# First layer's conditioning weights in eighths, summed by TensorE, with idle products in the planned pauses

## The chip, the cores and the metric

The kernel runs on one core of a Trainium2 chip. The metric is device time in microseconds (us): the median over the timed runs of one execution each.

## What is computed

A two-layer streaming encoder over x (2048 frames of 1024 channels, float32), with one conditioning vector c (1024). The part that matters here:

```python
c_act = jax.nn.silu(c)
for i in range(DEPTH):                                   # two layers
    cond = c_act @ ada_w[i] + ada_b[i]                   # ada_w[i]: 1024 x 3072
    shift, scale, gate = cond[:, None, :D], cond[:, None, D:2 * D], cond[:, None, 2 * D:]
    h = rmsnorm(x, norm_g[i]) * (1.0 + scale) + shift
    out = rglru_block(h, ...) if i == 0 else gated_deltanet_block(h, ...)
    x = x + gate * out
return rmsnorm(x, final_g)
```

Both blocks begin with a projection, h @ in_w (1024 x 2048 in the first layer). No projection of a layer can start before its shift and scale are known, and these are sums over all 1024 rows of a weight matrix: shift and scale of the first layer read 8 MB.

## The kernel before

**Tiling.** x is worked on in two halves of 1024 frames, each in two pieces of 512. h is kept with channels on partitions: eight column blocks k of 128 channels, each 128 x 512. The projection weights come in panels of 128 output columns (`raw`, 512 KB). Products are split for precision: weights into a high part `whi` (ScalarE, L701) and a rest `wlo` (VectorE, L707), h likewise into `hh` and `hl` (L622 or L625, and L627). One job is one panel against one piece of 512 frames: three products for each of eight blocks k, 24 matmuls of 128x128 by 128x512, accumulated in one PSUM bank (`mm`, L725). The first four jobs (two panels by two pieces) are interleaved, since each can go on only as far as the blocks of h are there.

**A block of h.** x's frames are loaded (L532), squared and summed by ScalarE (L506), the root taken on GpSimd (L289, L290), scaled by VectorE (L513), transposed by TensorE in blocks of four (`tph`, L547), then ScalarE applies scale and shift (`h`, L617, which waits for `cond` of block k) and the split follows.

**The conditioning columns.** The scale and the shift have to end up with channels on partitions, in `cond`. The 8 MB come in four quarters of 256 channels, each for both parts (part 1 is the scale, part 0 the shift), each in two halves of four row blocks: 16 transfers (`ada`, L346) of 512 KB. The two parts are summed in different ways:

- the scale in `first_pe_thread`: TensorE multiplies c, repeated over 32 columns (`c_bc`), with the raw weights, row blocks j and j+4 in output rows 32j to 32j+31 of one bank (`adaps`, L394); ScalarE copies the bank to `atmp` (L399), and a product with `corner`, a column of ones at rows 0, 32, 64 and 96, adds the four groups and turns 128 channels at a time into a column (L325).
- the shift in `first_dve_thread`: VectorE multiplies the first row block by c and accumulates seven more (`acc`, L418, L420); a product with `ones` adds over partitions (`adac`, L325).

`finish_columns` then adds the bias (L315) and makes g(1 + scale) of the scale (L318). TensorE starts with 40 products of the identity with itself into a bank that nobody reads (`rest`, L379).

**The order.** Nobody writes the order of the instructions by hand. Each piece of work is a generator (a thread of the program `Weave`) that yields the engine that it needs next with a cost in us, an event or a slot of a buffer; the planner always takes the thread that can start first by its own clock, and of equals the one with the higher priority. So costs, priorities and events fix the order in each engine's queue, and on the chip each engine runs its queue strictly in that order. All loads are issued by SP's queue. `SEEDS` scatters the costs by 1%, from another seed every 16 jobs: other seeds give another order for the rest of the program. Each engine's own waits on the chip come on top of the plan.

Of the kernel before, what the change touches and what calls it, by code (L numbers as in the profile page):

```python
# [9 lines left out]
F32 = mybir.dt.float32  # L10
# [3 lines left out]
ALU = mybir.AluOpType  # L14

S = 2048
D = 1024
P = 128
KT = D // P
T = 1024  # L20
NU = S // T
TC = 512
# [54 lines left out]
class Weave:  # L77
    def __init__(self):
        self.free = dict.fromkeys(("pe", "act", "dve", "pool", "sp", "dma"), 0.0)
        self.held = {"dve2": [], "pool2": []}  # L80
        self.table = "exp"
        self.landed, self.through = [0.0] * 8, 0.0
        self.scatter, self.jobs = random.Random(SEEDS[0]), 0
        self.threads = []
        self.now = 0.0

    def count(self):
# [16 lines left out]
    def put(self, slots, token):  # L104
        slots.freed[token] = self.now
# [20 lines left out]
    def engine(self, th, t, kind, dur, lag=None, table=None):  # L126

        e = th.last = kind.rstrip("2")
        if e != "pe":
            dur *= 1.0 + SPREAD * self.scatter.gauss(0.0, 1.0)  # L130
        if table is not None and table != self.table:
            t, self.table = t + TABLE, table
        if kind in SHARED:
            for a, b in self.held[SHARED[kind]][-6:]:
                if a <= t < b:
                    t = b
            self.held[kind].append((t, t + dur + (0.08 if e == "dve" else 0.0)))
        self.free[e] = t + dur
        th.t = t + dur + (LAG[e] if lag is None else lag)

# [36 lines left out]
def trunk_kernel(ctx, tc, x, head, small, ada0, ada_w, ada_b, final_g, w1, gate_w, ow1, w2, wab, ow2, out):  # L177
# [9 lines left out]
    pools = {}  # L187
# [10 lines left out]
    def flat(ap):  # L198
        return ap.rearrange("p a b -> p (a b)")
# [127 lines left out]
    H = TC // 2  # L327

    def first_loads_thread():

        yield ev("firstpanel")
        for q in range(4):
            if q == 1:
                yield ev("firstpanels")
            if q == 3:
                yield ev("loaded", (("in1", 0), 1))
            if q % 2 == 0:
                p = hp if q == 0 else pools["hc"]
                raws = [p.tile([P, KT, TC], F32, tag=f"h{'lh'[part]}{'BC'[q // 2]}", name=f"ada{part}{q}") for part in range(2)]
                raws = [flat(r).rearrange("p (a k c) -> p a k c", a=2, c=H) for r in raws]  # L340
            for part in range(2):
                w.set(ev("adaraw", part, q), raws[part][:, q % 2])
            for g in range(2):
                for part in (1, 0):
                    yield "sp", 1.3, False
                    sp.dma_start(out=raws[part][:, q % 2, 4 * g:4 * g + 4, :], in_=ada0[4 * part + q, :, 4 * g:4 * g + 4, :])  # L346
                    w.spawn(arrive_thread(ev("adaload", part, q, g)), 0)
            w.set(ev("adaissue", q))
# [28 lines left out]
    def idle_products(pt, n):  # L377
        for _ in range(n):
            pe.matmul(pt[:, 0:P], lhsT=ident, rhs=ident, start=True, stop=True)  # L379

    def first_pe_thread():

        rest = ps.tile([P, TC], F32, tag="mm", name="rest")
        idle_products(rest, 40)
        c_bc, ttok = yield ev("cbc")
        for q in range(4):
            raw = yield ev("adaraw", 1, q)
            ctok = yield slots["c"]
            pt = ps.tile([P, H], F32, tag="c", name="adaps")
            for g in range(2):  # L390
# [12 lines left out]
            yield from finish_columns(0, 1, 2 * q, 2, pt[:, 0:2])  # L403
            put("c", ctok)
        put("yf", ttok)

    def first_dve_thread():

        yield ev("c")
        for q in range(4):  # L410
            ttok = yield slots["tz"]
            acc = tile_([P, H], "tz", "acc")
            raw = yield ev("adaraw", 0, q)
# [7 lines left out]
            ctok = yield slots["c"]  # L421
            yield "pe", 0.5
            pt = ps.tile([P, 2], F32, tag="c", name="adac")
            columns_of(acc, pt, 2, ones[:, 0:1])
            put("tz", ttok)
            yield from finish_columns(0, 0, 2 * q, 2, pt)
            put("c", ctok)
        yield ev("cond", 0, 1, KT - 1)
        w.set(ev("ada"))

    def columns_thread():
        neg = tile_([P, KT], "tf1", "neg")
# [229 lines left out]
    def panels_thread():  # L662
        yield ev("small")
        ahead = []
        for name, panels, _ in plans:
            for m, p in enumerate(panels):
# [4 lines left out]
                    yield ev("owt", 1, 1)  # L671
                    yield ev("gates")
                if m == 0 and name == ("in1", 0):
                    yield ev("loaded", (("in1", 0), 0))
                    ahead.append((yield from panel_load(name, panels[0])))
                    w.set(ev("firstpanel"))
                    yield ev("adaissue", 0)
                    ahead.append((yield from panel_load(name, panels[1])))
                    w.set(ev("firstpanels"))
                if m in (2, len(panels) - 1) or m < 2 and name != ("in1", 0):  # L680
                    if name == ("in1", 0):
                        yield ev("adaissue", 3)
# [1031 lines left out]
    with tc.manual_schedule():  # L1714
# [20 lines left out]
        w.spawn(norm_thread((in1[0], 1), 0, x, TC, "B", [ev("adaissue", 2)], [ev("cond", 0, 1, 3), ev("cond", 0, 0, 3)],  # L1735
                            ("yh", "yh", "yl", "yl"), "tg"), 2)
        w.spawn(turned_thread((in1[1], 0), 0, x, T, "C", [ev("adaissue", 3), ev("split", (in1[0], 1), KT - 1)],
                              [ev("turned", (in1[1], 1))], [ev("ada")]), TP)
        w.spawn(turned_thread((in1[1], 1), 0, x, T + TC, "A", [ev("turned", (in1[1], 0))], [ev("loaded", (in1[1], 0))], [ev("free", in1[0], 0)]), TP)
        w.spawn(out_weights_thread(1, ow1, 0, 0.5, "B", [ev("free", in1[0], 1)], []), 3)  # L1740
# [31 lines left out]
def layout(**inputs):  # L1772
# [10 lines left out]
    def table(*parts):  # L1783
# [40 lines left out]
```

## Time and profile before

| | |
|---|---|
| median of 3 timed runs | 1838.78 us (1836.51 to 1843.77) |
| profiled execution | 1842.69 us |
| its span, first to last instruction | 1840.4 us |
| TensorE busy | 1808.1 us, 98% |
| VectorE busy | 1343.7 us, 73% |
| ScalarE busy | 1136.3 us, 62% |

The span is that of one profiled execution, and the views of the trace are about it. Busy time of TensorE is that of pipelined products whose ends are modelled, so two rows can overlap by some tenths of a us; the distance from one start to the next is the better price. A 32-bit product shows as two rows, one for each pass; products of the split parts show as one.

### The profile page before, as it was taken

Reading aid. Unit: us, or ns where it says so; the run is one execution under the profiler, and the core shown is the slowest. Engines: PE = TensorE matmul, PEld = TensorE weight load, DVE = VectorE, ACT = ScalarE, POOL = GpSimd, SP = SyncE. Lnnn points to the kernel's source line nnn. Section 1 sums busy time; section 2 is a strip of 40 time slices with the busy share of each in tenths; the row PEclk is TensorE's granted clock in tenths of the full one; section 3 lists DMA queues with packets and bytes.
Section 4 is the critical chain, followed back from the end, with each engine's and each line's share of the span. In section 5 each row is a group of like instructions: output and inputs, shape, how many; then the busy total and the mean of one; then the engine's idle time right before and its main releaser. Section 6 shows DMA issues by size and latency. Waiting matters only on the chain.

```text
span 1840.4 us, 31168 instructions
## 1 busy us (share of the span) xinstructions
PE 1808.1 (98%) x10350; PEld 1454.5 (79%) x10350; DVE 1343.7 (73%) x3113; ACT 1136.3 (62%) x2683; POOL 359.9 (20%) x895
## 2 busy tenths in 40 slices
PE   8999999999999999999999999999999999999998
PEld 6777776777788878787888788787888888778887
DVE  7889887777554747877788887677766776876653
ACT  4766766666212358686877676776787687664221
POOL 2112001000000003223333231232222232211100
PEclk8999999999999999999999999999999999999999
DMA  9567746555678735667677667456555565686741
GB/s 360 140 192 208 241 158 193 159 180 164 205 211 226 225 103 150 161 164 171 165 188 174 153 146 226 117 148 161 147 135 140 148 155 137 163 261 186 249 139 69
DMA packets 510424, 322.74 MB, mean 175 GB/s; under 512 B 369844, under 2 KB 437940, under 8 KB 510264
## 3 DMA queue, kind: packets, MB, share of 16 engines
q1 hardware_dynamic: 510264, 320.77, 62.7%
q8 instruction: 81, 1.33, 0.3%
q14 instruction: 79, 0.65, 0.1%
HBM read 219.93 MB, written 100.73 MB: 174 GB/s over the span
## 4 chain that ended last, share of the span: by engine, by line
PE 71%; DVE 10%; DMA 6%; ACT 5%; issue 4%; SPq 3%; POOL 1%; DVEq 0%; POOLq 0%; ACTq 0%
PE mm L725 39%; PE mmo L725 18%; PE pg L858 3%; DVE xf L778 2%; DMA raw<-in_w 2%; PE py L1451 1%; PE pS L1464 1%; PE pS L1463 1%; PE pp L1434 1%; PE pp L1435 1%; PE pqk L1284 1%; DVE tblk L1319 1%; PE pkk L1196 1%; DVE ttmp L1316 1%; SPq L1531 1%
## 5 line engine op out<-in xcount | busy, mean ns | idle before, releaser
L778 DVE SCALAR_TENSOR_TENSOR xf<-xe,small_s,xf 128x512 f32<-128x512 f32 x288 | 215.1, 751 | 49.9 <-ACT xf L1037 46.3
L701 ACT CAST whi<-raw 128x1024 fp32r<-128x1024 f32 x96 | 100.0, 1041 | 33.0 <-DMA raw<-in_w 29.6
L1316 DVE TENSOR_TENSOR ttmp<-blk,tblk 128x60 f32<-128x60 f32 (+24 forms) x496 | 104.7, 211 | 15.8 <-DMA blk<-blk_d 4.2
L1319 DVE TENSOR_TENSOR tblk<-tblk,ttmp 128x60 f32<-128x60 f32 (+24 forms) x496 | 105.9, 214 | 12.5
L725 PE MATMUL mm<-hh_('in2', 1)_11904,whi 128*128 128x512 f32 x256 | 104.0, 406 | 0.7 <-ACT tz L1052 0.7
L725 PE MATMUL mm<-hh_('in2', 1)_11629,whi 128*128 128x512 f32 x256 | 104.4, 408 | 0.1
L725 PE MATMUL mm<-hl_('in2', 1)_11905,whi 128*128 128x512 f32 x256 | 104.0, 406 | 0.0
L725 PE MATMUL mm<-hh_('in2', 1)_11629,wlo 128*128 128x512 f32 x256 | 103.7, 405 | 0.0
L725 PE MATMUL mm<-hh_('in2', 0)_5185,whi 128*128 128x512 f32 x256 | 103.6, 405 | 0.0
L725 PE MATMUL mm<-hh_('in2', 1)_11904,wlo 128*128 128x512 f32 x256 | 103.5, 404 | 0.0
L725 PE MATMUL mm<-hh_('in2', 0)_5074,wlo 128*128 128x512 f32 x256 | 103.4, 404 | 0.0
L725 PE MATMUL mm<-hl_('in2', 1)_11630,whi 128*128 128x512 f32 x256 | 103.4, 404 | 0.0
L725 PE MATMUL mm<-hh_('in2', 0)_5074,whi 128*128 128x512 f32 x256 | 103.3, 403 | 0.0
L725 PE MATMUL mm<-hh_('in2', 0)_5185,wlo 128*128 128x512 f32 x256 | 103.2, 403 | 0.0
L725 PE MATMUL mmo<-oh,oh 128*128 128x512 f32 (+1 forms) x264 | 103.0, 390 | 0.0
L725 PE MATMUL mm<-hl_('in2', 0)_5186,whi 128*128 128x512 f32 x256 | 102.9, 402 | 0.0
L725 PE MATMUL mm<-hl_('in2', 0)_5075,whi 128*128 128x512 f32 x256 | 102.8, 402 | 0.0
L725 PE MATMUL mmo<-ol,oh 128*128 128x512 f32 (+1 forms) x264 | 102.6, 388 | 0.0
L725 PE MATMUL mmo<-oh,ol 128*128 128x512 f32 (+1 forms) x264 | 102.4, 388 | 0.0
L725 PE MATMUL mmo<-oh,yl 128*128 128x512 f32 x256 | 100.9, 394 | 0.1
L725 PE MATMUL mmo<-oh,yh 128*128 128x512 f32 x256 | 100.8, 394 | 0.0
L725 PE MATMUL mmo<-ol,yh 128*128 128x512 f32 x256 | 100.8, 394 | 0.0
(321 smaller groups left out, 5315.6 us busy)
## 6 DMA issues: line engine op xcount, KB each, us to landing
raw<-in_w SPq DMA_DIRECT2D x96, 512.0 KB, 4.1
araw<-in_ada_w SPq DMA_DIRECT2D x32, 512.0 KB, 4.8
xt<-x_d SPq DMA_DIRECT2D x32, 512.0 KB, 6.0
xt_d<-xb SPq DMA_DIRECT2D x192, 64.0 KB, 2.6
xk<-xt_d SPq DMA_DIRECT2D x24, 512.0 KB, 5.8
xt<-in_x SPq DMA_DIRECT2D x16, 512.0 KB, 6.4
ada<-in_ada SPq DMA_DIRECT2D x16, 512.0 KB, 10.8
y_d<-tz SPq DMA_DIRECT2D x32, 256.0 KB, 3.4
```

The source lines that it names most:

```text
L701: act.copy(hi, raw)
L725: pe.matmul(pt, lhsT=lhs[a][:, k, :], rhs=rhs[b][:, k, :], start=(k == 0 and n == 0), stop=(k == KT - 1 and n == 2))
L778: dve.scalar_tensor_tensor(xf, xe[:, 1 + j:1 + j + TC], wc[:, j:j + 1], xf, ALU.mult, ALU.add)
L858: pe.matmul(pg, lhsT=gw[:, g, :], rhs=xf, start=True, stop=True)
L1196: pe.matmul(pkk[:, b, :], lhsT=kc, rhs=kc, start=True, stop=True)
L1284: pe.matmul(pqk[:, b, :], lhsT=kt[:, b * P:(b + 1) * P], rhs=qt[:, b * P:(b + 1) * P], start=True, stop=True)
L1316: dve.tensor_tensor(tmp, blk[:, j, j + 1:32].unsqueeze(2).to_broadcast([P, r, c_]), t[:, j, 0:c_].unsqueeze(1).to_broadcast([P, r, c_]), A ...
L1319: dve.tensor_tensor(t[:, j + 1:32, 0:c_], t[:, j + 1:32, 0:c_], tmp, ALU.subtract)
L1434: pe.matmul(pp[:, 0, :], lhsT=kc, rhs=S_, start=True, stop=True)
L1435: pe.matmul(pp[:, 1, :], lhsT=qc, rhs=S_, start=True, stop=True)
L1451: pe.matmul(py, lhsT=rm[:, b, :], rhs=zt, start=True, stop=True)
L1463: pe.matmul(pS[:, 0, :], lhsT=kd[:, b, :], rhs=yt, start=True, stop=True)
```

## The change

1. The weights come in eighths: 128 channels of one part with all eight row blocks, 16 transfers of 512 KB as before. `first_loads_thread` issues the first pair right behind x's first piece, then the first panel, a pair, the second panel, two pairs, x's second piece (which waited for three quarters before, and for four eighths now) and the last four pairs.
2. Both parts are summed by TensorE: two `first_pe_thread`, one for each part. An eighth is eight products of 32 x 128 in four column groups, a copy (ScalarE for the scale and the first shift, VectorE for the other seven), one product with `corner` and `finish_columns` for one column. `first_dve_thread` is gone.
3. Idle products: `warm_thread`, with the lowest priority, puts one wherever TensorE is free in the plan, until the first block of h is split. After that `engine` fills each planned pause of TensorE before 45 us of the plan with as many as fit, if an `adaps` bank is open to take them.
4. The seeds are others.

```diff
-SEEDS, SPREAD = (32, 45, 51, 36, 4, 54, 53, 16, 3, 25, 36, 8, 28, 14, 37, 0, 0), 0.01
+SEEDS, SPREAD = (59, 49, 32, 0, 2, 54, 53, 2, 57, 22, 53, 52, 51, 54, 27, 0, 0), 0.01
+IDLE = 45.0
...
+        if e == "pe" and self.idle and t < IDLE:
+            self.idle(int((t - self.free[e] - 0.1) / 0.23))
...
-        yield ev("firstpanel")
-        for q in range(4):
-            if q == 1:
+        yield ev("loaded", (("in1", 0), 0))
+        for e in range(8):
+            if e == 1:
+                yield ev("firstpanel")
+            if e == 2:
                 yield ev("firstpanels")
-            if q == 3:
+            if e == 4:
                 yield ev("loaded", (("in1", 0), 1))
...
-                    sp.dma_start(out=raws[part][:, q % 2, 4 * g:4 * g + 4, :], in_=ada0[4 * part + q, :, 4 * g:4 * g + 4, :])
+                sp.dma_start(out=raws[part][:, e % 4], in_=ada0[8 * part + e])
...
-    def first_pe_thread():
-
-        rest = ps.tile([P, TC], F32, tag="mm", name="rest")
-        idle_products(rest, 40)
+    def warm_thread(stop):
+
+        mtok = yield slots["mm"]
+        pt = ps.tile([P, TC], F32, tag="mm", name="warm")
+        while stop.t is None:
+            yield "pe", 0.43 if w.now < 7.0 else 0.23, 0.0
+            pe.matmul(pt[:, 0:P], lhsT=ident, rhs=ident, start=True, stop=True)
+        put("mm", mtok)
+        w.idle = idle_products
+
+    def idle_products(n):
+
+        if w.rest is not None:
+            for _ in range(n):
+                pe.matmul(w.rest[:, 3 * P:4 * P], lhsT=ident, rhs=ident, start=True, stop=True)
+
+    def first_pe_thread(part, other):
...
-            for g in range(2):
-                yield ev("adaload", 1, q, g)
-                yield "pe", 1.15 if q + g else 2.2, 0.0 if g == 0 else 0.2
-                for j in range(4):
-                    pe.matmul(pt[32 * j:32 * j + 32], lhsT=c_bc[:, 4 * g + j, :], rhs=raw[:, 4 * g + j, :],
-                              start=(g == 0), stop=(g == 1))
+            for k in range(KT):
+                pe.matmul(pt[32 * (k % 4):32 * (k % 4) + 32, 0:P], lhsT=c_bc[:, k], rhs=raw[:, k, :], start=(k < 4), stop=(k >= 4))
             xtok = yield slots["xr"]
-            yield "act", 0.36
-            tmp = tile_([P, H], "xr", "atmp")
-            act.copy(tmp, pt)
-            yield "pe", 0.5
-            columns_of(tmp, pt, 2, corner)
+            tmp = tile_([P, P], "xr", "atmp")
+            if part == 0 and e > 0:
+                yield "dve", 0.2
+                dve.tensor_copy(out=tmp, in_=pt[:, 0:P])
+            else:
+                yield "act", 0.2
+                act.copy(tmp, pt[:, 0:P])
+            yield "pe", 0.25, 0.3
+            pe.matmul(pt[:, 0:1], lhsT=tmp, rhs=corner, start=True, stop=True)
...
-    def first_dve_thread():
-
-        yield ev("c")
-        for q in range(4):
...
-            for k in range(KT):
-                yield ev("adaload", 0, q, k // 4)
-                yield "dve", 0.41
-                if k == 0:
-                    dve.tensor_scalar(acc, raw[:, 0], c_col[:, 0:1], None, ALU.mult)
-                else:
-                    dve.scalar_tensor_tensor(acc, raw[:, k], c_col[:, k:k + 1], acc, ALU.mult, ALU.add)
...
-        w.spawn(first_pe_thread(), 1)
-        w.spawn(first_dve_thread(), 0)
+        w.spawn(warm_thread(ev("split", (in1[0], 0), 0)), 20, 1.0)
+        w.spawn(first_pe_thread(1, 0), 1)
+        w.spawn(first_pe_thread(0, 1), 1)
...
-        "ada0": v["ada_w"][0, :, :2 * D].reshape(KT, P, 8, TC // 2).transpose(2, 1, 0, 3),
+        "ada0": v["ada_w"][0, :, :2 * D].reshape(KT, P, 16, P).transpose(2, 1, 0, 3),
```

The start of TensorE's queue before, up to the first weight product (each row: line, operation, output and operands, size of the output, count; `ada_182` holds quarters of the scale, `tph` are the transposes of x):

```order
L379 MATMUL rest<-ident 128x128 x40
L394 MATMUL adaps<-ada_182,c_bc 32x256 x4
L547 MATMUL tph<-ident,xt 128x128 x4
L394 MATMUL adaps<-ada_182,c_bc 32x256 x4
L547 MATMUL tph<-ident,xt 128x128 x8
L325 MATMUL adaps<-corner,atmp 128x1 x2
L547 MATMUL tph<-ident,xt 128x128 x4
L325 MATMUL adac<-ones,acc 128x1 x2
L394 MATMUL adaps<-ada_182,c_bc 32x256 x4
L547 MATMUL tph<-ident,xt 128x128 x8
L394 MATMUL adaps<-ada_182,c_bc 32x256 x4
L725 MATMUL mm<-hh_('in1', 0)_263,whi 128x512
```

The same start with the change (`ada_141` holds eighths of the scale, `ada_140` of the shift):

```order
L384 MATMUL warm<-ident 128x128 x35
L404 MATMUL adaps<-ada_141,c_bc 32x128 x8
L384 MATMUL warm<-ident 128x128 x3
L404 MATMUL adaps<-ada_140,c_bc 32x128 x8
L414 MATMUL adaps<-corner,atmp 128x1
L384 MATMUL warm<-ident 128x128
L541 MATMUL tph<-ident,xt 128x128 x4
L414 MATMUL adaps<-corner,atmp 128x1
L541 MATMUL tph<-ident,xt 128x128 x4
L384 MATMUL warm<-ident 128x128
L541 MATMUL tph<-ident,xt 128x128 x4
L404 MATMUL adaps<-ada_141,c_bc 32x128 x8
```

The first weight product stands six rows further on, behind the two eighths of the second pair, where it stood behind two quarters of the scale. Up to the first eighth of the second group (`ada_352`) the queue now holds 8 eighths, 8 column sums, 9 idle products besides the first 35, 8 blocks of four transposes and 24 weight products.

The end of the conditioning work in TensorE's queue before (`_263`, `_264` are h of the first piece, `_505`, `_506` of the second):

```order
L394 MATMUL adaps<-ada_254,c_bc 32x256 x4
L547 MATMUL tph<-ident,xt 128x128 x4
L725 MATMUL mm<-hl_('in1', 0)_264,whi 128x512
L725 MATMUL mm<-hh_('in1', 0)_263,wlo 128x512
L325 MATMUL adaps<-corner,atmp 128x1 x2
L725 MATMUL mm<-hh_('in1', 0)_263,whi 128x512
L725 MATMUL mm<-hl_('in1', 0)_264,whi 128x512
L725 MATMUL mm<-hh_('in1', 0)_263,wlo 128x512
L325 MATMUL adac<-ones,acc 128x1 x2
```

And with the change (`_270`, `_271` the first piece, `_527` the second):

```order
L404 MATMUL adaps<-ada_352,c_bc 32x128 x8
L414 MATMUL adaps<-corner,atmp 128x1
L719 MATMUL mm<-hh_('in1', 0)_527,whi 128x512
L719 MATMUL mm<-hh_('in1', 0)_270,whi 128x512
L719 MATMUL mm<-hl_('in1', 0)_271,whi 128x512
L414 MATMUL adaps<-corner,atmp 128x1
L404 MATMUL adaps<-ada_351,c_bc 32x128 x8
L719 MATMUL mm<-hh_('in1', 0)_270,wlo 128x512
L541 MATMUL tph<-ident,xt 128x128 x4
L719 MATMUL mm<-hh_('in1', 0)_270,whi 128x512
L414 MATMUL adaps<-corner,atmp 128x1
```

The last column sum stood behind 36 of the 96 weight products of the first four jobs and 9 of 16 blocks of transposes; it now stands behind 35 and 10. Between the second group's first eighth and it are 8 eighths, 8 column sums, 5 idle products, 11 weight products and 2 blocks. Ahead of it stood a VectorE accumulation; now it is a VectorE copy, which waits for the eighth that TensorE has just done.

## Rows read from the trace of the kernel before

**Rows 1.** The page: busy us (share of the span) and instructions of each engine.

```profile
PE 1808.1 (98%) x10350; PEld 1454.5 (79%) x10350; DVE 1343.7 (73%) x3113; ACT 1136.3 (62%) x2683; POOL 359.9 (20%) x895
```

**Rows 2.** Windows: stretch and length, busy us (instructions) by engine, PEclk, DMA share, GB/s.

```profile
13.37:45.41 32.04, 26.49 (x165) 17.73 (x165) 24.52 (x59) 13.76 (x24) 5.30 (x8) 0.84 0.97 389
36.00:45.41 9.41, 7.47 (x45) 4.36 (x46) 8.64 (x21) 4.13 (x8) 3.98 (x6) 1.00 0.84 337
45.41:66.69 21.28, 21.26 (x101) 16.09 (x102) 19.26 (x39) 15.79 (x26) 1.48 (x4) 1.00 0.11 31
66.69:120.00 53.31, 53.31 (x222) 41.34 (x221) 47.10 (x77) 38.58 (x53) 9.69 (x14) 1.00 0.75 206
66.69:1780.00 1713.31, 1694.87 (x9754) 1364.58 (x9753) 1266.13 (x2955) 1088.97 (x2596) 340.81 (x844) 1.00 0.64 176
```

**Rows 3.** The chain that ended last, 41 to 60 us: start us, us, what.

```profile
41.25 0.75 DVE xt L513
42.00 0.40 DVE acc L420
...
44.88 0.39 DVE acc L420
...
45.41 0.58 PE adac L325 x4
45.99 0.80 PE mm L725 x3
...
48.75 0.44 PE tph L547 x4
...
53.03 6.15 PE mm L725 x27
```

**Rows 4.** The conditioning transfers (L346): issue in ns, first and last start; landing.

```profile
L346 SPq DMA_DIRECT2D ada<-in_ada x16: 328/328/483, 4.3 to 28.8; - x16
...
DMA to landing us min/median/max: 7.8/10.8/11.6
```

**Rows 5.** Groups by line, 0 to 66.7 us: busy us, mean ns | idle before.

```profile
L420 DVE SCALAR_TENSOR_TENSOR acc<-ada,c_col,acc 128x256 f32<-128x256 f32 x28 | 13.5, 483 | 1.2 <-DMA ada<-in_ada 0.6
...
L399 ACT COPY atmp<-adaps 128x256 f32<-128x256 f32 x4 | 1.5, 374 | 8.1 <-PE adaps L394 8.1
...
L418 DVE TENSOR_SCALAR acc<-ada,c_col 128x256 f32<-128x256 f32 x4 | 1.4, 348 | 0.2 <-DMA ada<-in_ada 0.2
...
L315 DVE TENSOR_TENSOR cond<-adaps,head_s 128x2 f32<-128x2 f32 x4 | 0.6, 154 | 1.9 <-PE adaps L325 1.9
```

**Rows 6.** Windows of the idle products (L379) alone: PE, PEld, PEclk, DMA, GB/s.

```profile
1.52:7.25 5.73, 5.73 (x27) 5.73 (x28) 1.00 0.87 280
7.25:13.37 6.12, 6.12 (x55) 5.99 (x54) 1.00 1.02 404
```

**Rows 7.** Windows, columns as in rows 2.

```profile
20.00:35.00 15.00, 13.63 (x76) 9.71 (x77) 10.18 (x25) 7.21 (x13) 0.41 (x2) 0.66 1.03 410
```

**Rows 8.** Timeline, 41 to 46 us: start us, us, instruction, count.

```profile
41.49 0.16 PEld L394 LDWEIGHTS adaps<-ada,c_bc 128*32 128x32 f32 x8 [0.36 <-issue]
41.49 0.64 PE L394 MATMUL adaps<-ada,c_bc 128*32 128x256 f32 x8
...
42.06 0.66 PE L547 MATMUL tph<-ident,xt 128*128 128x128 f32 x4
...
45.85 0.48 PE L725 MATMUL mm<-hh_('in1', 0)_505,whi 128*128 128x512 f32 x1
```

**Rows 9.** Timeline of PE, 19 to 67 us: [idle before <- what ended it].

```profile
19.93 0.64 PE L394 MATMUL adaps<-ada,c_bc 128*32 128x256 f32 x8 [1.05 <-DMA ada<-in_ada]
21.78 1.97 PE L547 MATMUL tph<-ident,xt 128*128 128x128 f32 x8 [1.21 <-ACT h L617]
...
24.69 0.80 PE L725 MATMUL mm<-hh_('in1', 0)_263,whi 128*128 128x512 f32 x1
...
66.69 0.39 PE L725 MATMUL mm<-hh_('in1', 0)_263,whi 128*128 128x512 f32 x1
```

**Rows 10.** PE's waits, 66.69 to 1780 us: us in total, times, longest.

```profile
PE pg L858 <- DMA gw<-in_gate_w: 2.2, 1, 2.2
```

More of the change, by code (lines that the diff above doesn't have):

```diff
@@ L84, in __init__ @@
         self.threads = []
+        self.idle = self.rest = None
         self.now = 0.0
@@ L325, in columns_of @@
             pe.matmul(pt[:, q:q + 1], lhsT=acc[:, q * P:(q + 1) * P], rhs=weights, start=True, stop=True)
-    H = TC // 2
     def first_loads_thread():
-        yield ev("firstpanel")
-        for q in range(4):
-            if q == 1:
+        yield ev("loaded", (("in1", 0), 0))
[3 more added lines that the diff above has]
+            if e == 2:
                 yield ev("firstpanels")
-            if q == 3:
+            if e == 4:
                 yield ev("loaded", (("in1", 0), 1))
[L337 to L342, printed above, removed]
-            for g in range(2):
-                for part in (1, 0):
-                    yield "sp", 1.3, False
-                    sp.dma_start(out=raws[part][:, q % 2, 4 * g:4 * g + 4, :], in_=ada0[4 * part + q, :, 4 * g:4 * g + 4, :])
-                    w.spawn(arrive_thread(ev("adaload", part, q, g)), 0)
-            w.set(ev("adaissue", q))
+            if e % 4 == 0:
+                p = hp if e == 0 else pools["hc"]
+                raws = [p.tile([P, KT, TC], F32, tag=f"h{'lh'[part]}{'BC'[e // 4]}", name=f"ada{part}{e}") for part in range(2)]
+                raws = [flat(r).rearrange("p (a k c) -> p a k c", a=4, c=P) for r in raws]
+            for part in (1, 0):
+                yield "sp", 1.3, False
+                sp.dma_start(out=raws[part][:, e % 4], in_=ada0[8 * part + e])
+                w.spawn(arrive_thread(ev("adaload", part, e), raws[part][:, e % 4]), 0)
+            w.set(ev("adaissue", e))
     def arrive_thread(event, value=True):
@@ L375, in first_small_thread @@
         w.set(ev("cbc"), (c_bc, ttok))
-    def idle_products(pt, n):
-        for _ in range(n):
-            pe.matmul(pt[:, 0:P], lhsT=ident, rhs=ident, start=True, stop=True)
-    def first_pe_thread():
-        rest = ps.tile([P, TC], F32, tag="mm", name="rest")
-        idle_products(rest, 40)
+    def warm_thread(stop):
[3 more added lines that the diff above has]
+            yield "pe", 0.43 if w.now < 7.0 else 0.23, 0.0
+            pe.matmul(pt[:, 0:P], lhsT=ident, rhs=ident, start=True, stop=True)
+        put("mm", mtok)
+        w.idle = idle_products
@@ L385, in first_pe_thread @@
+    def idle_products(n):
[3 more added lines that the diff above has]
+    def first_pe_thread(part, other):
         c_bc, ttok = yield ev("cbc")
-        for q in range(4):
-            raw = yield ev("adaraw", 1, q)
+        for e in range(8):
+            raw = yield ev("adaload", part, e)
             ctok = yield slots["c"]
-            pt = ps.tile([P, H], F32, tag="c", name="adaps")
-            for g in range(2):
-                yield ev("adaload", 1, q, g)
-                yield "pe", 1.15 if q + g else 2.2, 0.0 if g == 0 else 0.2
-                for j in range(4):
-                    pe.matmul(pt[32 * j:32 * j + 32], lhsT=c_bc[:, 4 * g + j, :], rhs=raw[:, 4 * g + j, :],
-                              start=(g == 0), stop=(g == 1))
-            xtok = yield slots["xr"]
-            yield "act", 0.36
-            tmp = tile_([P, H], "xr", "atmp")
-            act.copy(tmp, pt)
-            yield "pe", 0.5
-            columns_of(tmp, pt, 2, corner)
+            yield "pe", 0.46, 0.3
+            pt = ps.tile([P, TC], F32, tag="c", name="adaps")
+            w.rest = pt
+            for k in range(KT):
+                pe.matmul(pt[32 * (k % 4):32 * (k % 4) + 32, 0:P], lhsT=c_bc[:, k], rhs=raw[:, k, :], start=(k < 4), stop=(k >= 4))
+            xtok = yield slots["xr"]
+            tmp = tile_([P, P], "xr", "atmp")
[7 more added lines that the diff above has]
+            pe.matmul(pt[:, 0:1], lhsT=tmp, rhs=corner, start=True, stop=True)
@@ L402, in first_pe_thread @@
             put("xr", xtok)
-            yield from finish_columns(0, 1, 2 * q, 2, pt[:, 0:2])
+            yield from finish_columns(0, part, e, 1, pt[:, 0:1])
+            if w.rest is pt:
+                w.rest = None
             put("c", ctok)
-        put("yf", ttok)
-    def first_dve_thread():
-        yield ev("c")
[L410 to L413, printed above, removed]
-            for k in range(KT):
-                yield ev("adaload", 0, q, k // 4)
-                yield "dve", 0.41
-                if k == 0:
-                    dve.tensor_scalar(acc, raw[:, 0], c_col[:, 0:1], None, ALU.mult)
-                else:
-                    dve.scalar_tensor_tensor(acc, raw[:, k], c_col[:, k:k + 1], acc, ALU.mult, ALU.add)
[L421 to L429, printed above, removed]
@@ L431, in columns_thread @@
+        yield ev("cond", 0, other, KT - 1)
+        if part == 1:
+            put("yf", ttok)
+            w.set(ev("ada"))
     def columns_thread():
@@ L673, in panels_thread @@
                 if m == 0 and name == ("in1", 0):
-                    yield ev("loaded", (("in1", 0), 0))
+                    yield ev("adaissue", 0)
                     ahead.append((yield from panel_load(name, panels[0])))
                     w.set(ev("firstpanel"))
-                    yield ev("adaissue", 0)
+                    yield ev("adaissue", 1)
                     ahead.append((yield from panel_load(name, panels[1])))
@@ L681, in panels_thread @@
                     if name == ("in1", 0):
-                        yield ev("adaissue", 3)
+                        yield ev("adaissue", 7)
                     ahead.append((yield from panel_load(name, p)))
@@ L1734, in trunk_kernel @@
         w.spawn(rows_thread(), 4)
-        w.spawn(norm_thread((in1[0], 1), 0, x, TC, "B", [ev("adaissue", 2)], [ev("cond", 0, 1, 3), ev("cond", 0, 0, 3)],
+        w.spawn(norm_thread((in1[0], 1), 0, x, TC, "B", [ev("adaissue", 3)], [ev("cond", 0, 1, 3), ev("cond", 0, 0, 3)],
                             ("yh", "yh", "yl", "yl"), "tg"), 2)
-        w.spawn(turned_thread((in1[1], 0), 0, x, T, "C", [ev("adaissue", 3), ev("split", (in1[0], 1), KT - 1)],
+        w.spawn(turned_thread((in1[1], 0), 0, x, T, "C", [ev("adaissue", 7), ev("split", (in1[0], 1), KT - 1)],
                               [ev("turned", (in1[1], 1))], [ev("ada")]), TP)
```

## Prediction

> **What bounds the kernel now.** I first read where each engine is busy: TensorE 98% of the span, VectorE 73%, ScalarE 62% [rows 1]. A change at the start is therefore worth the TensorE time that it frees there, if that is not lost again. Next, the stretches [rows 2]. From 13.37 us (the last of the 40 idle products) to 45.41 us, TensorE works 26.49 of 32.04 us; from 45.41 us to 66.69 us, where the fifth job begins [rows 9], 21.26 of 21.28; up to 120 us all of it; up to 1780 us 1694.87 of 1713.31. So from 45.41 us on TensorE hardly waits. The question is what it waits for before, and how much work is left at that moment.
>
> The chain of work shows it [rows 3]: before 45.41 us it runs through VectorE, over the row scales of x's second half (L513) and the weighted sum of the shift columns (L420), into the column sums `adac` (L325). From 45.99 us on it is TensorE alone. Was the data late? The last conditioning transfer was issued at 28.8 us, and such a transfer takes 10.8 us (7.8 to 11.6) to land [rows 4], so it was there at 39.6 us (40.4 at the latest). The last run of accumulations starts at 42.00 us in the chain: VectorE, busy 8.64 of the last 9.41 us, and not the transfers, holds the tail [rows 2, 3].
>
> **The change, part by part.**
>
> *VectorE and ScalarE.* 28 accumulations of 483 ns and four multiplications of 348 ns go, 14.9 us [rows 5]. In come seven copies of 128x128 from PSUM; the trace has none. A two-column operation from PSUM takes 0.15 us on VectorE, ScalarE's copy of twice the columns 0.37 [rows 5]; between these I take 0.25, 1.8 us together. So the VectorE end of the chain goes. ScalarE swaps four copies of 0.37 us for nine, at 0.25 each: +0.8 us, in a stretch where it is idle for 18 of 32 us [rows 2].
>
> *Transfers.* 16 pieces of 0.5 MB stay 16. In the order of SP's queue x's second half moves ahead of four half quarters. The last piece keeps its place, so it lands at 39.6 us again; the piece that opens the second group of eighths comes seven transfers sooner. At the 410 GB/s that DMA moves here [rows 7] a transfer of 524 KB takes 1.28 us: it lands at 39.6 - 9.0 = 30.6 us.
>
> *TensorE, the prices.* An eighth is 8 products of 128 columns, 16 passes; a half quarter was 4 products of 256, 8 passes, in 0.64 us, and the next operation started 0.57 us behind its start [rows 8]. The streamed columns are the same, with four groups of 32 output rows at a time. If that overlap holds, an eighth costs 0.6 us. If it fails, each pass costs what a pass of the idle products costs: 55 of them start in the 6.12 us behind 7.25 us [rows 6], 111 ns each, so 1.78 us. I take 0.6, since eight loads of 32 columns took only 0.16 us [rows 8]. Against me speaks the Trainium skill (TensorE: Matmul & The Clock Gate, section Back-to-back issue gap): it puts a sustained stream of load and product pairs at 81 ns a pair for 128 columns, by which, as an estimate, an eighth is 1.3 us and the kernel ends near 1847. The trace's idle pairs are slower still than that, but its column groups overlap.
> Two column sums held TensorE for 0.44 us (45.41 to 45.85) [rows 3, 8]; one: 0.3 (0.22 to 0.44). A block of four transposes takes 0.44, a weight product 6.15/27 = 0.228 [rows 3]. An idle product is two passes, 0.22; the first 27 passes took 5.73 us, twice as long each, though no lower clock is recorded for them [rows 6].
>
> *TensorE, the sum.* The 35 products of `warm` at the start are 70 passes: 27 until 7.25 us, 43 x 0.111 = 4.8 us more, so they end at 12.0 us. From there to the second group of eighths the order holds 8 eighths (4.8), 8 column sums (2.4), 9 idle products (2.0), 8 blocks (3.5) and 24 weight products (5.5): 18.2 us, to 30.2 us, just when the next piece lands (30.6). From there to the last column sum: 8 eighths (4.8), 8 sums (2.4), 5 idle products (1.1), 11 weight products (2.5), 2 blocks (0.9), 11.7 us: 41.9 us with no wait. By the data alone it is 39.6 + 0.6 + 0.23 + 0.44 + 0.23 + 0.3 = 41.4 us. TensorE is now the later of the two. It will not be free of waits: before, they were 5.5 us of this stretch, two of them over 1 us between 18 and 22 us, for a transfer and for ScalarE [rows 2, 9]. In the new order ScalarE puts the four squares of x's second half between the split of columns 3 and 4, for which products wait. I put 1.5 us (0.4 to 4.5) for all waits: the last column sum ends at 43.4 us, where it ended at 45.99.
>
> *What is left then.* 61 of 96 weight products and 6 blocks, against 60 and 7: 0.23 - 0.44 = -0.2 us. So 43.4 - 45.99 - 0.2 = **-2.8 us** (-4 to +0.5). The first weight product comes much sooner than now (24.69 us [rows 9]), near 18 us; most of that only moves waits behind it.
>
> *The rest of the program.* TensorE is full until 120 us, with VectorE at 88% and the transfers at 75% [rows 2], so what follows starts sooner with it. The other seeds redraw the order of all that is behind; by the two orders the kinds and counts of instructions stay, but for four more ScalarE table loads. Behind 66.69 us TensorE waits 18.44 us [rows 2], the longest time, 2.2 us, for a gate-weight transfer [rows 10]. I cost the new order at nothing, with 4 us either way.
>
> The profiled execution took 1842.69 us, 2.3 above its span and 3.9 above the median of the three timed runs. On its own time the sum gives 1839.9; against the median, 1838.8 - 2.8 = **1836.0 us**.
>
> **The rivals.**
> *The clock falls (the gain is lost).* From 20 to 35 us the mean granted clock was 0.66, part of the time at the lower level of 1.2 GHz: 15 x 0.34 = 5.1 us of TensorE's time [rows 7], right after the two long waits [rows 9]. It cost little then, since TensorE had to wait anyway. The new order has 29.9 us of work in a stretch of 31, so the same fall costs 5.1 us less the 1.0 us of waits that it covers: 43.4 + 4.1, +1.3 us in all, 1840. For it: idle products fill the planned pauses, not those that a late transfer makes. Against: products of weights begin 6 us sooner and the pauses are shorter. It decides from 2.8 us lost, 5.6 us at half clock.
> *Eighths do not overlap (slower).* 16 x (1.78 - 0.6) = 18.9 us on TensorE's path, less 2.8: 1855. From 0.78 us for an eighth the gain is gone, from 1.35 us the kernel is slower by over 0.5%. Against it: the 0.64 us of the half quarter. The pair rate of the Trainium skill's TensorE page (same section) lies between the two.
> *The gain is not carried.* If later waits grow by as much as TensorE arrives sooner: 1838.8. For it: VectorE at 88%; against: a TensorE without a wait until 120 us.
> *The redrawn order decides.* If a third of the later 18.4 us goes, 1836 - 6 = 1830; if half, 1827; likewise upwards.
>
> **How the numbers follow.** Forecast 0.56 (its own range 1832 to 1840); not carried 0.12; clock 0.15; redrawn order by 6 us or more 0.11; eighths that do not overlap, or a clock that stays low through most of the head (24 us of it are needed), 0.06. The range from 1830 to 1844.5 leaves out most of the redrawn order, the slow eighths and a little of the clock. 0.5%, 9.2 us, is about what this measurement can tell from no change: below 1829.6 lies a lucky order (0.08), above 1848 the last case and an unlucky one (0.06), between them 0.86.
>
> **What would show it.** Right: the last column sum near 43 us, the first weight product near 18, the fifth job's first product near 64 us instead of 66.69, a clock of 1.00 from 10 to 45 us, some 0.64 us for the products of an eighth. Wrong: an eighth above 0.8 us, TensorE at the low clock while it is busy, waits for the copies `atmp` between eighths, or a later stretch that differs by more than 3 us.

## The result and the profile after

The changed kernel takes 1847.47 us (median of 7, 1846.3 to 1854.87), the kernel before 1838.73 us (7, 1836.51 to 1843.77): ratio 1.005, interval 1.0036 to 1.0064. So it is slower by 8.7 us, where 1836.0 us was forecast and the range ended at 1844.5. The profiled execution of after took 1846.65 us.

The page of after, row of the busy times, and its windows (columns as in [rows 2]), which answer to [rows 1, 2]:

```profile
PE 1812.9 (98%) x10560; PEld 1461.5 (79%) x10560; DVE 1329.9 (72%) x3100; ACT 1143.0 (62%) x2692; POOL 358.8 (19%) x895
```

```profile
13.37:45.41 32.04, 30.21 (x374) 23.22 (x373) 16.74 (x48) 16.90 (x31) 3.62 (x8) 1.00 0.97 387
36.00:45.41 9.41, 9.28 (x129) 7.00 (x122) 5.74 (x20) 4.12 (x8) 0.00 (x0) 1.00 0.84 336
45.41:66.69 21.28, 21.28 (x99) 16.38 (x99) 19.67 (x39) 16.09 (x27) 2.49 (x5) 1.00 0.15 41
...
1000.00:1200.00 200.00, 192.80 (x1300) 154.73 (x1299) 149.42 (x439) 139.67 (x402) 51.90 (x124) 0.99 0.59 152
```

VectorE has lost its accumulations (16.74 us busy in the head for 24.52), TensorE works 30.21 us of it, and its granted clock is 1.00 throughout. TensorE's timeline of after in the head answers to [rows 8, 9]:

```profile
18.43 0.64 PE L404 MATMUL adaps<-ada,c_bc 128*32 128x128 f32 x16
19.00 0.50 PE L719 MATMUL mm<-hh_('in1', 0)_270,whi 128*128 128x512 f32 x1
...
33.22 0.71 PE L392 MATMUL adaps<-ident 128*128 128x128 f32 x4 [0.38 <-ACT atmp L412]
33.77 0.28 PE L414 MATMUL adaps<-corner,atmp 128*128 128x1 f32 x2
33.98 0.64 PE L404 MATMUL adaps<-ada,c_bc 128*32 128x128 f32 x16
35.03 0.71 PE L392 MATMUL adaps<-ident 128*128 128x128 f32 x4 [0.41 <-DVE atmp L409]
35.68 0.64 PE L404 MATMUL adaps<-ada,c_bc 128*32 128x128 f32 x16
...
39.28 0.49 PE L719 MATMUL mm<-hh_('in1', 0)_270,whi 128*128 128x512 f32 x1
39.60 0.40 PE L719 MATMUL mm<-hl_('in1', 0)_271,whi 128*128 128x512 f32 x1
39.84 0.39 PE L719 MATMUL mm<-hh_('in1', 0)_270,wlo 128*128 128x512 f32 x1
40.06 0.28 PE L414 MATMUL adaps<-corner,atmp 128*128 128x1 f32 x2
...
45.12 0.28 PE L414 MATMUL adaps<-corner,atmp 128*128 128x1 f32 x2
...
65.39 0.40 PE L719 MATMUL mm<-hh_('in1', 0)_270,whi 128*128 128x512 f32 x1
```

The first parts behave much as forecast: 0.64 us for an eighth's 16 passes, the first weight product at 19.00 us (24.69 before, near 18 forecast). The fifth job starts at 65.39 us, 1.3 us sooner than in [rows 9], where 64 was forecast. But the last column sum starts at 45.12 us, against 45.41 before. One reason stands in the rows: the idle products of a planned pause (L392) write the `adaps` bank whose copy is running, and are released by that copy (`<-ACT atmp`, `<-DVE atmp`). They run behind the pause, not in it: 0.71 us for four passes ahead of the next column sum or eighth.

So after leads by 1.3 us at the fifth job and still ends 4.3 us behind before's profiled execution (spans 1844.7 and 1840.4). It changes sides in one stretch: from 1000 to 1200 us TensorE works 192.80 us (row above), in before 196.79:

```profile
1000.00:1200.00 200.00, 196.79 (x1336) 160.06 (x1335) 154.59 (x450) 145.06 (x420) 52.77 (x132) 1.00 0.62 159
```

What happens there in after is shown by SP's queue, the chain of waits and TensorE's timeline, three views of the same 20 us:

```profile
1097.63 1.90 SPq L596 DMA_DIRECT2D xk<-xt_d  x3
1099.63 0.92 SPq L1049 DMA_DIRECT2D z_d<-tz  x2
```

```profile
1099.63 7.84 DMA z_d<-tz
...
1107.55 0.61 ACT tz L1046
...
1108.20 4.00 PE mm L719 x11
```

```profile
1105.26 0.39 PE L719 MATMUL mm<-hh_('in2', 0)_5187,wlo 128*128 128x512 f32 x1
1108.20 0.50 PE L719 MATMUL mm<-hh_('in2', 0)_5187,whi 128*128 128x512 f32 x1 [2.55 <-ACT tz L1046]
...
1109.46 0.60 PE L719 MATMUL mm<-hh_('in2', 0)_5187,wlo 128*128 128x512 f32 x1
1109.86 0.63 PE L719 MATMUL mm<-hh_('in2', 0)_5187,whi 128*128 128x512 f32 x1
```

Three reloads of `xk` stand ahead of two stores of `z_d`. A store lands 7.84 us after its issue; the next `tz` can only then be written, and it releases the PSUM bank for which the product at 1108.20 us waits, 2.55 us. 1.3 us behind the start of that product the products take 0.6 us each: the granted clock is 0.50 for 3.4 us. The same place in before:

```profile
1101.72 0.37 SPq L1055 DMA_DIRECT2D z_d<-tz  x1
1102.13 2.31 SPq L602 DMA_DIRECT2D xk<-xt_d  x3
1104.55 0.40 SPq L1055 DMA_DIRECT2D z_d<-tz  x1
```

One store goes ahead of the reloads, and TensorE has no such wait (its longest from 1080 to 1114 us is 1.43 us, for another operand). The head did not change this queue; the redrawn order did.

### The profile page after: what moved, and what is told of

The parts are those of the page before. It is cut to its first block, busy times and chain, and to the rows that moved or that the text cites. A ratio compares the mean times of both kernels' runs of the same rounds, so it can differ in the third digit from the quotient of the medians.

```text
span 1844.7 us, 31580 instructions
## 1 busy us (share of the span) xinstructions
PE 1812.9 (98%) x10560; PEld 1461.5 (79%) x10560; DVE 1329.9 (72%) x3100; ACT 1143.0 (62%) x2692; POOL 358.8 (19%) x895
## 4 chain that ended last, share of the span: by engine, by line
PE 74%; DVE 9%; ACT 6%; DMA 5%; issue 2%; SPq 2%; POOL 0%; DVEq 0%; POOLq 0%; ACTq 0%
PE mm L719 42%; PE mmo L719 16%; PE pg L852 3%; DVE xf L772 1%; PE py L1445 1%; PE pqk L1278 1%; PE pp L1428 1%; PE pS L1457 1%; PE pS L1458 1%; PE pp L1429 1%; DMA oraw<-in_ow 1%; DVE tblk L1313 1%; PE pkk L1190 1%; DVE ttmp L1310 1%; DMA raw<-in_w 1%
## 5 line engine op out<-in xcount | busy, mean ns | idle before, releaser
L719 PE MATMUL mm<-hh_('in2', 0)_5187,whi 128*128 128x512 f32 x256 | 103.3, 403 | 3.2 <-ACT tz L1046 3.2
L719 PE MATMUL mm<-hh_('in2', 0)_5187,wlo 128*128 128x512 f32 x256 | 104.5, 408 | 0.0
L719 PE MATMUL mm<-hl_('in2', 1)_11740,whi 128*128 128x512 f32 x256 | 104.4, 408 | 0.0
L719 PE MATMUL mm<-hh_('in2', 1)_12016,wlo 128*128 128x512 f32 x256 | 104.3, 407 | 0.0
L719 PE MATMUL mm<-hh_('in2', 1)_11739,whi 128*128 128x512 f32 x256 | 103.6, 404 | 0.7 <-ACT tz L1046 0.7
L719 PE MATMUL mm<-hl_('in2', 0)_5299,whi 128*128 128x512 f32 x256 | 104.1, 407 | 0.0
L719 PE MATMUL mm<-hl_('in2', 1)_12017,whi 128*128 128x512 f32 x256 | 103.8, 406 | 0.0
L719 PE MATMUL mm<-hh_('in2', 0)_5298,whi 128*128 128x512 f32 x256 | 103.7, 405 | 0.0
L719 PE MATMUL mm<-hh_('in2', 1)_11739,wlo 128*128 128x512 f32 x256 | 103.7, 405 | 0.0
L719 PE MATMUL mm<-hl_('in2', 0)_5188,whi 128*128 128x512 f32 x256 | 103.6, 405 | 0.0
## 6 DMA issues: line engine op xcount, KB each, us to landing
ada<-in_ada SPq DMA_DIRECT2D x16, 512.0 KB, 10.2
```

The source lines that it names most:

```text
L719: pe.matmul(pt, lhsT=lhs[a][:, k, :], rhs=rhs[b][:, k, :], start=(k == 0 and n == 0), stop=(k == KT - 1 and n == 2))
```

## The experiments

**Theory:** the redrawn order loses the time, and the head is worth little. **Rivals:** the new head itself costs the time later on (its idle products, or its lead that meets other transfers); or the forecast's base, the profiled execution of before, had an unusual head.

The first four kernels part seeds, head and idle products.

*e1* and *e2* exchange the line of seeds between the two kernels. The diff is that of e1, the changed kernel with the old line; e2 is the kernel before with the new line, the reverse:

```diff
-SEEDS, SPREAD = (59, 49, 32, 0, 2, 54, 53, 2, 57, 22, 53, 52, 51, 54, 27, 0, 0), 0.01
+SEEDS, SPREAD = (32, 45, 51, 36, 4, 54, 53, 16, 3, 25, 36, 8, 28, 14, 37, 0, 0), 0.01
```

> The changed kernel with the old table of seeds. Theory A (the order behind the first jobs, redrawn by plan and seeds, decides; the first jobs themselves gain 1 to 3 us): away from the changed kernel's 1847, somewhere between 1830 and 1843, with the fifth job's first product still near 65.4 us. Theory B (eighths and idle products carry a cost of their own that comes due later, whatever the order): 1845 to 1849.

> The kernel before with the new table of seeds and nothing else. Theory A: the order alone moves the time by several us, 1840 to 1850, with the first 60 us about as in the kernel before. Theory B: within 2 us of the kernel before, 1837 to 1841.

*e3* issues no idle product at all, in the order of the changed kernel:

```diff
             yield "pe", 0.43 if w.now < 7.0 else 0.23, 0.0
-            pe.matmul(pt[:, 0:P], lhsT=ident, rhs=ident, start=True, stop=True)
...
     def idle_products(n):

-        if w.rest is not None:
-            for _ in range(n):
-                pe.matmul(w.rest[:, 3 * P:4 * P], lhsT=ident, rhs=ident, start=True, stop=True)
+        pass
```

> The changed kernel in which no idle product is issued at all (neither warm nor in the pauses); the plan, and with it the order of all else, is the same. Theory A: the granted clock falls for part of the first 45 us and the fifth job starts 2 to 6 us later, 1848 to 1853. Theory B, if the idle products are what costs: below 1845.

*e4* keeps the changed kernel's order to about 1000 us and draws the rest anew:

```diff
-SEEDS, SPREAD = (59, 49, 32, 0, 2, 54, 53, 2, 57, 22, 53, 52, 51, 54, 27, 0, 0), 0.01
+SEEDS, SPREAD = (59, 49, 32, 0, 2, 54, 53, 2, 57, 1, 1, 1, 1, 1, 1, 0, 0), 0.01
```

> The changed kernel with other seeds from the tenth entry on: the queues are word for word the same up to some 1000 us, where the changed kernel was 3 us ahead of the kernel before. Theory A: 3 us ahead at 1000 us, and then another result, anywhere from 1836 to 1850, away from 1847 by more than 2 us. Theory B: 1846 to 1849.

All four are slower than before (1837.45 us on that chip): e1 1847.04 us, ratio 1.0055 (1.0038 to 1.0072); e2 1848.88, 1.0063 (1.0044 to 1.0082); e3 1845.97, 1.0042 (1.0028 to 1.0057); e4 1855.08, 1.0098 (1.0083 to 1.0113). The old head with the new seeds is as slow as the changed kernel: a redrawn order alone can cost as much, though e2's order is not the changed kernel's own. The old seeds do not bring the time back either. e1's time lies where the rival put it; but behind another head the old seeds draw another order, which e7 below tells apart. Without idle products the loss stays. And a fresh draw behind 1000 us alone costs 0.5% more.

Seeds, then, do not hold an order fast. The next four kernels record the order in which one kernel's work was picked, and replay it behind another's head, from the fifth job on:

```diff
-            best = None
-            for th in self.threads:
+            best = self.replay()
+            for th in self.threads if best is None else ():
```

`replay` gives the next piece of the recorded order once five jobs have begun. The traces bear it out: behind the fifth job the instructions of e5, e7 and e8 stand in the order of before on every engine, those of e6 in the order of after. *e5* has the new head and before's order behind it, *e6* the old head and after's order, *e7* e1's head and before's order, *e8* e3's head without idle products and before's order.

> The changed kernel up to its fifth job, and behind it every engine's queue in the order of the kernel before (the planner's picks of the kernel before are replayed, so the last 8142 of TensorE's 8390 instructions stand as they stood). Theory A (the first jobs gain, the redrawn order behind them loses): 1 to 3 us faster than the kernel before, 1835 to 1837.5. Theory B (the eighths and idle products cost something that comes due later): 1845 to 1849 as the changed kernel.

> The reverse: the kernel before up to its fifth job, then every queue in the order of the changed kernel. Theory A: slower than the changed kernel by what the head gained there, 1847 to 1850. Theory B: within 2 us of the kernel before, 1836 to 1840.

> As the first of these four, but with the head that the old seeds gave the changed kernel (fifth job 2.8 us sooner than before instead of 1.3), and the old queue behind it. Theory A: 2 to 4 us faster than the kernel before, 1834 to 1836. Theory B: 1845 to 1849.

> As the first of these four, without any idle product: its head brought the fifth job 2.1 us sooner than before. Theory A: 1 to 3 us faster than the kernel before, and not slower than the first of the four: the idle products buy nothing. Theory B, with idle products as the cost: faster than the first of the four by over 3 us.

Measured (before 1839.02 us): e5 1842.13 us, ratio 1.0022 (1.0010 to 1.0034); e6 1846.67, 1.0042 (1.0025 to 1.0058); e7 1840.90, 1.0012 (1.0000 to 1.0024); e8 1843.34, 1.0022 (1.0011 to 1.0032). The order of after costs 0.4% under the old head; the new head costs 0.1 to 0.2% under the old order, and never gains. For e5, e7 and e8 neither theory had the number: the first expected 1834 to 1838 us, since the head was to gain, the second 1845 us and more (for e8, less than e5 by over 3). The windows from 1000 to 1200 us follow the order, whatever the head; these are e6 (new order) and e7 (old):

```profile
1000.00:1200.00 200.00, 192.25 (x1290) 154.20 (x1289) 148.04 (x434) 138.57 (x400) 51.03 (x123) 0.98 0.59 152
```

```profile
1000.00:1200.00 200.00, 196.37 (x1338) 159.86 (x1337) 153.79 (x448) 146.43 (x423) 52.50 (x132) 1.00 0.61 158
```

*e9* is the changed kernel with one move in its recorded order, the stores ahead of the reloads on SP's queue (rows by its place):

```diff
-SPq xk<-xt_d x3
 SPq z_d<-tz x2
+SPq xk<-xt_d x3
```

> The changed kernel with one move in its order: the two stores of z_d that stand behind three reloads of xk on the sync engine's queue near 1098 us now stand ahead of them; nothing else moves. Theory A (the redrawn order loses the time, here at this queue): TensorE's wait of 2.55 us at 1108 us and the 3.4 us of half clock behind it are gone, and the time falls by 3 to 5 us from the changed kernel's, to about 1843 us (ratio about 1.002). Rival (the wait is a symptom and the time is lost again further on): 1846 to 1848 us, ratio 1.004 to 1.005.

It takes 1842.11 us, ratio 1.0029 (1.0019 to 1.0039) to before at 1837.68 us: 2 in 1000, about 4 us, below the changed kernel's 1.005, whose interval it overlaps a little (1.0036 to 1.0064). Its queue, the store's landing and the wait of TensorE from 1080 to 1112 us (longest last), and its window:

```profile
1097.54 2.84 SPq L1380 DMA_DIRECT2D z_d<-tz  x2
1100.43 1.49 SPq L927 DMA_DIRECT2D xk<-xt_d  x3
```

```profile
DMA to landing us min/median/max: 5.1/5.2/5.3
```

```profile
PE mm L1050 <- ACT tz L1377: 1.4, 2, 0.7
```

```profile
1000.00:1200.00 200.00, 194.45 (x1322) 156.39 (x1321) 150.57 (x440) 143.14 (x408) 53.36 (x127) 1.00 0.58 152
```

The longest wait falls from 2.6 to 0.7 us, and this trace has no half clock there. So by the medians this one place is some two fifths of the loss. Two more waits from 1000 to 1200 us stand in after, e6 and e9 and not in r1 below: for `qt` (0.9 to 2.2 us) and for `yt` (1.2 us); r1 has one for `ac` (1.99 us) that they lack.

Does the half clock belong to the wait? In r3 below, the changed kernel again, both stand at this place; in e3, which has the same order, a longer wait has no half clock behind it. The rows are those of r3, then of e3, each with a window:

```profile
1109.49 0.80 PE L719 MATMUL mm<-hh_('in2', 0)_5187,whi 128*128 128x512 f32 x1 [3.06 <-ACT tz L1046]
```

```profile
1109.20:1112.60 3.40, 3.11 (x7) 2.49 (x8) 1.47 (x7) 0.24 (x1) 0.00 (x0) 0.50 1.01 252
```

```profile
1110.44 0.50 PE L716 MATMUL mm<-hh_('in2', 0)_5138,whi 128*128 128x512 f32 x1 [3.16 <-ACT tz L1043]
```

```profile
1110.44:1113.84 3.40, 3.40 (x15) 2.82 (x16) 1.10 (x6) 0.00 (x0) 0.00 (x0) 1.00 0.95 218
```

So the wait comes with the order, and the half clock comes with it in some executions and not in others.

*e10* and *e11* ask how special the order of before is: every entry of its table is set to 1, or to 2.

```diff
-SEEDS, SPREAD = (32, 45, 51, 36, 4, 54, 53, 16, 3, 25, 36, 8, 28, 14, 37, 0, 0), 0.01
+SEEDS, SPREAD = (1, 1, 1, 1, 1, 1, 1, 1, 1, 1, 1, 1, 1, 1, 1, 1, 1), 0.01
```

> The kernel before with every entry of its table of seeds set to 1: same work, another draw of the order from the first job on. Theory A (the table of before is a lucky draw, and any other draw costs what the changed kernel's does): 1844 to 1857 us, ratio 1.003 to 1.01. Rival (draws scatter evenly about the kernel before): 1836 to 1842 us, ratio 0.998 to 1.002.

> As the run with seeds 1, with every entry set to 2: a third draw. Theory A: 1844 to 1857 us, ratio 1.003 to 1.01. Rival: 1836 to 1842 us.

1857.63 us, ratio 1.0114 (1.0093 to 1.0135), and 1859.56 us, 1.0120 (1.0096 to 1.0144). Same work, 20 us more, and not from the head (e10's last column sum starts at 43.32 us): the order of before is much better than these plain draws. The page of e10 tells where they go:

```profile
PE 1817.4 (98%) x10350; PEld 1458.5 (78%) x10350; DVE 1342.0 (72%) x3113; ACT 1139.7 (61%) x2685; POOL 352.4 (19%) x895
```

The same 10350 products in a span of 1858.5 us. Against r1 below (1803.9 us busy in 1834.0) they are busy for 13.5 us more, and TensorE idles 41.1 us for 30.1. So in these two executions 11.0 of 24.5 us are waits. The granted clock accounts for some 10 us of the longer busy time: up to its last 5 us e10 is at 0.50 for 27.2 us (3.4 in the head, then 6.8 from 862.2 and from 927.0, 3.4 from 1049.9, 1118.2 and 1558.5 us), r1 for 6.8 us, all in the head. Where the other 3 us come from stays open.

*e12* is the kernel before with 1 idle product ahead of the first job in place of 40:

```diff
-        idle_products(rest, 40)
+        idle_products(rest, 1)
```

> The kernel before, queue unchanged, with 1 idle product ahead of its first job in place of 40: a small disturbance of the head alone. If the order of before is fitted to its own head, so that any other head costs it: +1 to +4 us, 1840 to 1843 us, ratio 1.001 to 1.002. Rival (a lead or a lag in the head has no effect further on): within 1 us of the kernel before, ratio 0.9995 to 1.0005.

1837.47 us, ratio 1.0001 (0.9989 to 1.0013): this disturbed head costs nothing, the rival's case. Yet its last column sum starts at 42.32 us and its fifth job at 63.60 us, 3.1 us sooner than in [rows 3, 9]. Was the profiled head of before a usual one? *r1* and *r2* are the kernel before again, *r3* the changed kernel again, without any edit, each profiled once.

> The kernel before, unchanged, profiled again. If its first profile showed a late head: the last column sum of the conditioning starts at 42 to 43.5 us in place of 45.41, the fifth job at about 64 us in place of 66.7, the stretch at half clock is shorter than 10 us. Rival (the head of before is always so): 45 to 45.8 us and 66.5 to 67 us.

> As the run before it, a third profile of the kernel before: the same two expectations.

> The changed kernel, unchanged, profiled again. If its head is steady, as its clock is: last column sum at 44.5 to 45.5 us, fifth job at 65 to 65.6 us, and the wait of TensorE for tz at 1108 us of 2 to 3 us again. Rival (it scatters as the old head does): 42.5 to 45.5 us.

They take 1836.16, 1836.75 and 1848.43 us. The last column sum and the fifth job in r1, then the last column sum in r2 and r3:

```profile
43.29 0.58 PE L325 MATMUL adac<-ones,acc 128*128 128x1 f32 x4 [1.07 <-DVE cond L318]
...
64.56 0.39 PE L725 MATMUL mm<-hh_('in1', 0)_263,whi 128*128 128x512 f32 x1
```

```profile
42.81 0.58 PE L325 MATMUL adac<-ones,acc 128*128 128x1 f32 x4 [1.09 <-DVE cond L318]
```

```profile
44.95 0.28 PE L414 MATMUL adaps<-corner,atmp 128*128 128x1 f32 x2
```

The fifth job starts at 64.06 us in r2 and 65.21 us in r3. The head of before scatters by 2.6 us, the new one less: its last column sum starts between 44.48 and 45.21 us in after, r3, e4, e5 and e9. And in two of its three profiles the old head is 0.8 to 1.3 us ahead of after. The scatter goes with the clock. Windows over the stretch of low clock in the profile of before, in r1 and in r2, each with its own length:

```profile
20.90:31.10 10.20, 9.32 (x41) 6.92 (x45) 5.66 (x16) 3.31 (x6) 0.00 (x0) 0.50 1.03 410
```

```profile
19.10:25.90 6.80, 5.42 (x27) 3.17 (x28) 5.67 (x11) 3.12 (x6) 0.00 (x0) 0.50 1.03 410
```

```profile
21.40:24.80 3.40, 3.19 (x17) 2.05 (x18) 3.21 (x7) 1.99 (x5) 0.00 (x0) 0.51 1.03 418
```

The head and the later stretch, side by side (start of the last column sum and of the fifth job; TensorE's busy time from 1000 to 1200 us):

| kernel | column sum | fifth job | busy |
|---|---|---|---|
| before / r1 / r2 | 45.41 / 43.29 / 42.81 | 66.69 / 64.56 / 64.06 | 196.79 / 196.56 / 197.11 |
| after / r3 | 45.12 / 44.95 | 65.39 / 65.21 | 192.80 / 192.01 |
| e5, new head, old order | 44.48 | 64.75 | 195.69 |
| e6, old head, new order | 42.85 | 64.12 | 192.25 |
| e3, no idle products, new order | 44.34 | 65.32 | 193.08 |
| e8, no idle products, old order | 42.55 | 62.81 | 197.00 |
| e9, one move | 45.06 | 65.32 | 194.45 |

e3 and e8 have the same head and lie 1.8 us apart. Their rows show why: the same eight transposes, first in e3, then in e8, and a window over the start of e3:

```profile
18.02 1.97 PE L538 MATMUL tph<-ident,xt 128*128 128x128 f32 x8
```

```profile
17.11 1.09 PE L869 MATMUL tph<-ident,xt 128*128 128x128 f32 x8
```

```profile
11.31:19.78 8.47, 8.37 (x73) 6.76 (x73) 3.64 (x7) 4.08 (x7) 1.16 (x2) 1.00 1.03 411
```

Without idle products ahead of them the first operations take about twice their time, until 19.8 us in e3 and some 16.5 us in e8, although the granted clock reads 1.00. Their first two eighths together take 2.26 and 2.27 us, where after's first takes 0.64 us. The first 27 passes of [rows 6] were slow in the same way.

## Why the prediction was wrong

The step that failed is the one on the rest of the program: "I cost the new order at nothing, with 4 us either way." It was worth some 8 us: e6, the old head with the new order, takes 1846.67 us for 1839.02. A second one failed too, and it alone would have left no gain: "43.4 - 45.99".

- *Prices of the new operations.* Right. Eighth 0.64 us for 0.6 forecast, a column sum 0.28 for 0.3, the copies 0.29 us on VectorE and 0.27 on ScalarE for 0.25. The prediction's estimate of 1.3 us for an eighth came from the 81 ns a pair that the Trainium skill states (TensorE: Matmul & The Clock Gate, Back-to-back issue gap); the row has 16 passes in 0.64 us, 40 ns each, in four column groups. The time came out near the 1847 us of that estimate by luck, not for that reason.
- *Clock in the head.* Right: 1.00 from 10 to 45 us. But this reading does not show what the idle products do: in e3, without any, it is 1.00 there as well, and yet the first operations take twice their time. The idle products ahead of the first eighth spare that; the later ones, in the pauses, bought nothing that shows.
- *TensorE's tail, "the last column sum ends at 43.4 us".* Too early by 2.0 us (45.12 + 0.28 = 45.40). The term that was mis-sized is the weight products. From one start to the next, after's 35 take 10.1 us where 8.0 were forecast: 0.228 us was the price of one in a row, and beside another operation it is 0.3 and more (39.28 to 39.60 us in the rows of after). The 14 idle products take 4.0 us for 3.1, the column sums 3.4 for 4.8; the waits, 1.8 us for 1.5, hold 0.8 us for copies ahead of idle products. The five idle products of the second group cost 1.4 us: from its first eighth to the end of the last sum after, r3, e5 and e9 need 13.2 us, e3 and e8 11.8.
- *"43.4 - 45.99 - 0.2 = -2.8 us".* The base was an accident. 45.99 us is the end in one execution, with 10.2 us of half clock in its head and a time 3.9 us above the median. In r1 and r2 the sum ends at 43.87 and 43.39 us. Against these the new head ends its last sum 1.5 to 2.0 us later, and starts the fifth job 0.8 to 1.3 us later, not 2.8 sooner. That the profiled time was above the median stood in the prediction; it was subtracted from the total, and the place where it arose was not looked for.
- *The redrawn order.* The rival "likewise upwards" is what happened. Between r1 and after the spans differ by 10.7 us. The rows give: 0.8 us at the fifth job; TensorE's busy time less by 1.1 us from 66.69 to 1000 us (925.49 for 926.58), by 3.8 from 1000 to 1200 (192.80 for 196.56), by 0.7 from 1200 to 1780 (573.35 for 574.04); and three stretches of 3.4 us at half clock, from 856.9, 1109.5 and 1662.4 us, where r1 has none behind its head, 5.1 us. Together 11.5 us. In r3 the three lie at 863.4, 1109.2 and 1259.4 us, so only the second lies at the same place in both.
- *Sizes.* "Four us either way" was bounded by the waits that before had left, 18.4 us. A draw could only take from these, but it can add without such a bound, and a longer wait can bring a stretch of half clock. e10 and e11 show 20 us.

What stays open: e5 and e9 have 0.2 to 0.3% left, 3 to 5 us, of which their heads show one. The profiled executions of e9 (1839.59 us) and e5 (1839.72) are the quickest and the second quickest of their 12, 2.5 and 2.4 us below the medians, and show no half clock from 10 us to 1780; what the others have is not in a trace. And e8, whose fifth job starts 1.3 to 1.8 us sooner than in r1 and r2, still ends 0.2% behind before. Its trace shows where the lead goes: TensorE works 5.2 us less than in r1 from 66.69 to 1780 us (1691.95 for 1697.19), and two stretches of 3.4 us of half clock, from 596.9 and 856.3 us, start 0.9 to 1.0 us behind the ends of waits of 1.63 and 1.38 us that r1 does not have. Why the same order waits longer behind this head was not settled. No kernel tried here beats before.

## What to carry to other kernels

When an edit makes a planner draw a new order, forecast that draw apart from the edit: an order that is better than a plain draw loses when it is drawn again (three other draws of the kernel before, e2, e10 and e11, cost 0.6 to 1.2%), and a kernel that redraws it without the edit gives a first idea how much. Measure an edit behind a replayed order before judging it. And do not take a gain against one profiled execution that lies above the median: profile it again, and see which stretch scatters. Compare the time of the same instruction too: a granted clock of 1.00 did not mean that products ran at full pace.

## What was not expected of the hardware

- In after a TensorE wait of 2.55 us was followed by 3.4 us at half clock, from 1.3 us behind its end. In r3, with a wait of 3.06 us at the same place, the half clock began 0.3 us before the wait ended (0.50 from 1109.2 to 1112.6 us). In e3 a wait of 3.16 us there had none behind it, nor had the 0.7 us in e9. So such a wait does not always bring it.
- Without idle products the first operations took about twice their time (e3 to 19.8 us, e8 to some 16.5 us) at a granted clock that reads 1.00.
- The same program had 10.2, 6.8 and 3.4 us of half clock in its head in three executions, and the fifth job followed, 66.69, 64.56 and 64.06 us.
- 39 idle products less ahead of the first job (e12) changed nothing in the time, although TensorE then waited 10.1 us for the first weights, and the first two half quarters took 1.08 us each where r1 has 0.64.
